# Nearest-neighbour upsampling on one core: the first load as two DMAs over alternate partitions

## The chip, the cores and the metric

The kernel runs on one core of one Trainium2 chip. The metric is the device time of one execution in microseconds (us). Three runs of the kernel before gave 196.85, 196.99 and 197.22 us; their median, 196.99 us, is the time that the change is measured against.

Of the core's engines the kernel uses VectorE (DVE in the profile) and ScalarE (ACT) for copies inside the on-chip memory, and SyncE (SP) to issue DMAs, the transfers between the device memory and the on-chip memory. A DMA is carried out by 16 DMA engines that work beside the compute engines.

## The reference

The input `x` has the shape 16 x 64 x 64 x 64 in float32 (16.78 MB). Each element is repeated twice along the height and twice along the width, so that the output is 16 x 64 x 128 x 128 (67.11 MB):

```python
for i in range(new_h):
    for j in range(new_w):
        result[:, :, i, j] = x[:, :, i // scale_factor, j // scale_factor]
```

Nothing is computed with the numbers. Each is read once and written four times.

## The kernel before, in words

**Layout.** All 65,536 image rows (16 x 64 x 64, of 64 elements each) are dealt out to the 128 partitions of the on-chip memory: partition p holds R = 512 rows in succession, 128 KB of the input, and the output that belongs to them is 512 KB in succession. One tile, `mem`, takes the whole work: the input lies at its end (`xt`), and the space ahead of it (79 rows' worth of output, `FREE`) and the space of input rows that are used up hold expanded rows.

**Loads.** Four DMAs on SP's queue (lines 192 to 197) bring the input in, cut by rows: rows 0 to 31 (`HEAD`, 8 KB per partition, 1.05 MB in all), rows 32 to 255 and 256 to 479 (56 KB per partition, 7.34 MB each), and rows 480 to 511 (1.05 MB). Each of them covers all 128 partitions. They wait for nothing.

**Nine steps.** The rows are worked on in nine blocks (`rows`, line 181: 52, 40, 52, 63, 52, 64, 63, 63 and 63). For a block, VectorE expands the first 9/16 of its rows (line 215) and ScalarE the rest (line 216) into a region `u` of `mem`, and one DMA on SP's queue stores the region (line 217). The regions of even blocks lie at the start of `mem`, those of odd blocks just ahead of the input rows that are still to be used, so that a block's copies wait for the store that last read their region and for the rows that they read. The first store is also made to wait for the third load, `loads[-2]` (lines 218 to 226), so that stores begin when nearly all of the input is in.

**Order.** The tile framework puts a wait on each instruction for what it reads or overwrites. One step written by hand bears on the change: `begin_before_barrier` (line 11) takes the first `EARLY` instructions of SP, asserts that each is a DMA without a wait, and moves them ahead of the barrier at which the program's engines meet at its start. With `EARLY = 4` those are the four loads. `close_early` (line 74) shapes the end: the closing barrier and most of the clearing of semaphores happen while the last stores are still under way, and the last instruction, on SP, waits for the last store to land.

A DMA has its own semaphore, and what depends on it waits for that. The semaphores for DMAs are eight, used in turn: DMA number n takes number n modulo 8.

Of the kernel before, what the change touches and what calls it, by code (L numbers as in the profile page):

```python
# [6 lines left out]

EARLY = 4  # L10


def begin_before_barrier(nc):
# [5 lines left out]
    sp = mybir.EngineType.SP  # L19
    loads = [i for i in body.instructions if i.engine == sp][:EARLY]  # L20
    for load in loads:
# [132 lines left out]
@with_exitstack  # L154
def kernel(
    ctx: ExitStack,
    tc: tile.TileContext,
    x: bass.AP,
    scale_factor: int,
    out: bass.AP,  # L160
):
    nc = tc.nc
    nc.at_finalize(begin_before_barrier)
    nc.at_finalize(close_early)
    P = nc.NUM_PARTITIONS
    s = int(scale_factor)
    B, C, H, W = x.shape
    R = B * C * H // P
    fdt = x.dtype

    xp = x.rearrange("b c h w -> (b c h) w").rearrange("(p r) w -> p r w", p=P)
    op = out.rearrange("b c (h hd) w -> (b c h) (hd w)", hd=s).rearrange(
        "(p r) w -> p r w", p=P
    )

    rows = [52, 40, 52, 63, 52, 64, 63, 63, 63]
    GROW = s * s
    FREE = 79
    WF = FREE * GROW * W
    assert sum(rows) == R
    mem_pool = ctx.enter_context(tc.tile_pool(name="mem", bufs=1))
    mem = mem_pool.tile([P, WF + R * W], fdt, name="mem")
    xt = mem[:, WF:].rearrange("p (r w) -> p r w", r=R)

    HEAD = 32
    cuts = [0, HEAD, R // 2, R - 32, R]
    loads = [
        nc.sync.dma_start(out=xt[:, lo:hi], in_=xp[:, lo:hi])  # L195
        for lo, hi in zip(cuts, cuts[1:])
    ]

    def expanded(r0, r1):
        return (  # L200
            xt[:, r0:r1].unsqueeze(2).unsqueeze(4).to_broadcast([P, r1 - r0, s, W, s])
        )

    r0 = 0
    before = (0, 0)
    for n, k in enumerate(rows):
        size = k * GROW * W
        at = 0 if n % 2 == 0 else WF + r0 * W - size
        assert at >= before[1] or at + size <= before[0]
        before = (at, at + size)  # L210
        u = mem[:, at : at + size].rearrange(
            "p (k a w b) -> p k a w b", k=k, a=s, w=W
        )
        kv = k * 9 // 16
        nc.vector.tensor_copy(out=u[:, :kv], in_=expanded(r0, r0 + kv))  # L215
        nc.scalar.copy(out=u[:, kv:], in_=expanded(r0 + kv, r0 + k))  # L216
        store = nc.sync.dma_start(out=op[:, r0 : r0 + k, :], in_=u)  # L217
        if n == 0:
            tc.add_manual_dep(
                store.ins,  # L220
                loads[-2].ins.name,
                mybir.DependencyInfo(
                    mybir.DependencyClass.Sync, mybir.DependencyReason.DATA
                ),
                reason="stores begin as the loads end",
            )
        r0 += k
# [35 lines left out]
```

## Time and profile before

| | |
|---|---|
| median of three runs | 196.99 us (196.85 to 197.22) |
| the profiled execution | 197.0 us |
| its span, first to last instruction | 195.7 us |
| bytes moved by DMA | 83.89 MB, 429 GB/s over the span |
| share of 16 DMA engines' span taken by packets | 99.3% |
| VectorE busy | 69.7 us (36%), 9 copies |
| ScalarE busy | 51.4 us (26%), 9 copies and a table load |
| issue of the four loads on SP | 0.00 to 2.02 us; 383 to 632 ns each, median 434 |
| first VectorE copy begins | 4.59 us |
| first store issued | 38.52 us |

The profiled execution agrees with the median of the runs, and 1.3 us of it lie outside its span. The span runs from SP's first DMA issue to the end of the last wait on SP. Where the profile gives the DMA share over a short stretch, a packet counts wholly in the slice in which it begins; a value over 1 followed by a zero is such a packet. Each packet of data is one partition's piece of one DMA; the packets under 512 B are the signals that tell a semaphore of a DMA's end, 16 for each DMA.

### The profile page before, as it was taken

What the parts mean: (1) busy time and instruction counts of PE and PEld (TensorE: products, weight loads), DVE (VectorE), ACT (ScalarE), POOL (GpSimd) and SP (SyncE); (2) the same over time, 40 slices, a digit from 0 to 9 for tenths busy, and PEclk for the clock granted to TensorE, in tenths of its full rate; (3) what the DMA queues carried; (4) which work ended last, traced back from release to release, by engine and by line L of the source; (5) the groups of instructions that cost most, each with busy time, mean ns of one, the idle gap of its engine ahead of it and who ended that gap; (6) DMA issues with size and microseconds to landing.
All of it is one profiled execution on the core that took longest, in us unless ns stands there. A gap on an engine that the chain in (4) does not pass through costs nothing.

```text
span 195.7 us, 105 instructions
## 1 busy us (share of the span) xinstructions
DVE 69.7 (36%) x9; ACT 51.4 (26%) x10; POOL 0.2 (0%) x4
## 2 busy tenths in 40 slices
DVE  0950600000039299069008205930692079100000
ACT  0000595000036093064910006666000074000000
POOL 0000000000000000000000000000000000000000
DMA  9899889799899989899999899999999999999994
GB/s 402 375 481 457 375 375 563 310 440 523 348 442 452 526 348 512 359 422 422 422 422 523 348 523 429 429 429 429 422 422 422 422 422 422 528 514 422 435 422 211
DMA packets 1872, 83.89 MB, mean 429 GB/s; under 512 B 208, under 2 KB 208, under 8 KB 208
## 3 DMA queue, kind: packets, MB, share of 16 engines
q1 hardware_dynamic: 1872, 83.89, 99.3%
HBM read 16.78 MB, written 67.11 MB: 429 GB/s over the span
## 4 chain that ended last, share of the span: by engine, by line
DMA 67%; DVE 18%; SPq 0%; issue 0%; DVEq 0%
DMA out_dram<-mem 48%; DMA mem<-in_x_dram 19%; DVE mem L215 18%; SPq L195 0%; DVEq L215 0%; SPq L217 0%
## 5 line engine op out<-in xcount | busy, mean ns | idle before, releaser
L215 DVE COPY mem<-mem 128x8960 f32<-128x8960 f32 (+3 forms) x9 | 69.7, 7740 | 97.5 <-DMA out_dram<-mem 83.9
L216 ACT COPY mem<-mem 128x7168 f32<-128x7168 f32 (+2 forms) x9 | 50.1, 5572 | 90.8 <-DMA out_dram<-mem 84.3
L216 ACT ACT_TABLE_LOAD x1 | 1.3, 1283 | 21.6 <-DMA mem<-in_x_dram 21.6
L244 POOL MEMSET const-bfloat16-1.0<- 128x1 bf16 x1 | 0.1, 102 | 0.0
L244 POOL MEMSET const-uint8-127<- 128x1 uint8 x1 | 0.1, 102 | 0.0
L244 POOL MEMSET const-float32-0.0<- 128x1 f32 x1 | 0.1, 99 | 0.2 <-issue 0.2
L244 POOL MEMSET const-float32-1.0<- 128x1 f32 x1 | 0.1, 99 | 0.0
## 6 DMA issues: line engine op xcount, KB each, us to landing
out_dram<-mem SPq DMA_DIRECT2D x4, 8064.0 KB, 28.4
out_dram<-mem SPq DMA_DIRECT2D x3, 6656.0 KB, 19.7
mem<-in_x_dram SPq DMA_DIRECT2D x2, 7168.0 KB, 29.3
out_dram<-mem SPq DMA_DIRECT2D x1, 5120.0 KB, 29.8
mem<-in_x_dram SPq DMA_DIRECT2D x2, 1024.0 KB, 22.1
out_dram<-mem SPq DMA_DIRECT2D x1, 29.9
```

What stands on the lines that cost most here:

```text
L215: nc.vector.tensor_copy(out=u[:, :kv], in_=expanded(r0, r0 + kv))
L216: nc.scalar.copy(out=u[:, kv:], in_=expanded(r0 + kv, r0 + k))
L244: nc = _bacc.Bacc("TRN2", target_bir_lowering=False, num_devices=1)
```

## The change

The load of rows 0 to 31 becomes two DMAs. The first covers the even partitions (0, 2, ... 126), the second the odd ones (1, 3, ... 127), 64 pieces of 8 KB each. The other three loads stay as they are, as do the copies and the stores. `loads` now holds only those three, and `loads[-2]` is still the load of rows 256 to 479. `EARLY` goes from 4 to 5, so that all five loads go ahead of the opening barrier.

```diff
-EARLY = 4
+EARLY = 5
...
     HEAD = 32
     cuts = [0, HEAD, R // 2, R - 32, R]
+    for odd in range(2):
+        nc.sync.dma_start(out=xt[odd::2, :HEAD], in_=xp[odd::2, :HEAD])
     loads = [
         nc.sync.dma_start(out=xt[:, lo:hi], in_=xp[:, lo:hi])
-        for lo, hi in zip(cuts, cuts[1:])
+        for lo, hi in zip(cuts[1:], cuts[2:])
     ]
```

The order of instructions on VectorE, ScalarE and GpSimd is unchanged. The first copy on VectorE now waits for two DMAs in place of one, the first use of ScalarE likewise waits for one more, the first store names two more semaphores among its waits and the second store one fewer. SP issues 14 DMAs in place of 13.

## Prediction

> **What bounds the kernel now.** I read the page's engine rows, its DMA queue row, the chain that ended last, then the waits, and last short stretches of time at the start, where the change lies.
>
> ```profile
> span 195.7 us, 105 instructions
> DVE 69.7 (36%) x9; ACT 51.4 (26%) x10; POOL 0.2 (0%) x4
> DMA  9899889799899989899999899999999999999994
> ...
> q1 hardware_dynamic: 1872, 83.89, 99.3%
> HBM read 16.78 MB, written 67.11 MB: 429 GB/s over the span
> ...
> DMA 67%; DVE 18%; SPq 0%; issue 0%; DVEq 0%
> ```
>
> No compute engine is busy for 40% of the span, but packets fill 99.3% of the 16 DMA engines' time. The chain gives VectorE 18%, but that is time in which the queues still hold another store: the DMA row has no slice under 7 before the last. So the kernel ends when the DMA engines have moved 83.89 MB, and an edit is worth what it changes of three things: when they start, how fast they run, and how long the last landing takes.
>
> ```profile
> core 0: us, DVE busy (x) ACT busy (x) POOL busy (x), PEclk, DMA share, GB/s
> 0.00:1.00 1.00, 0.00 (x0) 0.00 (x0) 0.20 (x4) 1.00 0.00 0
> 1.00:2.00 1.00, 0.00 (x0) 0.00 (x0) 0.00 (x0) 1.00 1.01 229
> 2.00:3.00 1.00, 0.00 (x0) 0.00 (x0) 0.00 (x0) 1.00 1.01 426
> 3.00:4.00 1.00, 0.00 (x0) 0.00 (x0) 0.00 (x0) 1.00 1.06 451
> 4.00:8.00 4.00, 3.41 (x1) 0.00 (x0) 0.00 (x0) 1.00 1.03 444
> ...
> 140.00:194.00 54.00, 17.67 (x2) 6.16 (x1) 0.00 (x0) 1.00 1.01 440
> ```
>
> These stretches show the start: nothing moves for 1 us after the first issue, then a microsecond at 229 GB/s in which the engines are all busy but their packets slow, and from 2 us on the steady rate. Loads (2 to 38 us) and stores (after 41) run at the same rate, and pieces of 8 KB at the same as pieces of 64 KB. What limits an engine is thus common to reading and writing device memory and is no cost per packet: it is the engine itself (429 / 16 = 26.8 GB/s each) or its way into the on-chip memory.
>
> ```profile
> L195 SPq DMA_DIRECT2D mem<-in_x_dram x4: 383/434/632, 0.0 to 1.4; - x4
> ...
> DVE mem L215 <- DMA mem<-in_x_dram: 13.6, 2, 9.0
> ACT L216 <- DMA mem<-in_x_dram: 21.6, 1, 21.6
> ...
> SPq L217 <- DMA mem<-in_x_dram: 36.1, 1, 36.1
> ```
>
> The first row is the issue of the loads on SP (shortest, median, longest in ns). The others are waits (total us, times, longest): VectorE, after its first copy, idles 9.0 us for the second load; SP waits 36.1 us until the third load lands and the first store may go.
>
> **The change part by part.**
>
> *One more issue on SP, ahead of the barrier.* One issue by the median row is 0.43 us. The other loads are issued that much later, and the barrier opens at about 2.5 us in place of 2.1. The second part of the head is issued at about 0.4 us, and by the row of the first load (issue at 0, data from 1.0 us) its data can move from about 1.4 us; half the head takes 0.52 MB / 429 GB/s = 1.2 us and is not through before 2.2. So the gap between them is covered by some 0.8 us. The next load, needed at about 4 us, is issued by 0.9. The barrier covers nothing that is needed before 4.59 us, where VectorE's first copy starts. If the cover were gone, each of these would cost up to its 0.43 us. Price: 0.
>
> *One more semaphore and its waits.* VectorE's first copy and ScalarE's first instruction get one more wait. The chain shows what waits cost to pass: 0.08 us lie between the third load's landing at 38.44 us and the first store's issue at 38.52. VectorE has 9.0 us of idle time behind the copy. The first store's added waits are for DMAs that ended 34 us earlier; if they delay it by 0.1 us, the fourth load, 1.05 MB or 2.4 us of queued work, covers it. The second store loses a wait, and its issue too lies behind a queued store. The 16 extra end-of-DMA packets: the 208 that exist lie inside 99.3% of busy time at an overall 429 GB/s, so the whole difference to the 440 of the late stretch, spread over 13 DMAs, would be 195.7 x (1 - 429/440) / 13 = 0.38 us per DMA. That bound holds the start and the tail too, so the true price is far lower. Price: 0, with 0.38 as upper end.
>
> *An earlier start of the streams.* The first DMA has 64 pieces to prepare in place of 128. If preparing them sets the start, half of the first issue of 383 ns, 0.19 us, comes off. If the start is a fixed delay, nothing does. A gain above 0.38 us would need the whole issue to vanish. I take 0.1 us, bounds 0 and -0.38.
>
> *How the head's 1.05 MB spread over the ways into memory.* This is the term that decides. Every DMA in the trace covers all 128 partitions in sequence, so no row shows a transfer that leaves out every other partition. Lower bound: the spread over 16 engines and their ways into memory stays even, each half takes 0.52 MB / 429 GB/s, together 2.44 us as now: 0. [...] I take +2.1, between these two, and the side of sharing rather than of the even spread. The nearest row, the load of all partitions, speaks for the even spread, but the equal rate of loads and stores leaves a limit at the way into memory possible, and the partition pattern is the one thing that changes for it. This is a judgement, and the lower bound stays in the range.
>
> [...]
>
> *Sum.* 0 + 0 - 0.1 + 2.1 = +2.0 us. The transfers are back to back from here to the end, the queues never run empty, and no engine idles for want of the delayed data except where it idles already; the delay goes whole into the end. Profiled execution: 195.7 + 2.0 = 197.7 of span, + 1.3 outside it = 199.0 us. That execution's 197.0 is the median of the runs, so 199.0 stands for those too.
>
> **The rivals.**
>
> *Even spread, hidden edit (the other side).* The halves move at full rate and only the start counts: 196.99 - 0.1, between 196.6 and 197.35 us. For it: 99.3% of busy time and covers everywhere. Against it: nothing that a row shows, only the untested pattern. It decides if the stretch from 2 to 4 us stays above 400 GB/s.
>
> *An earlier start that counts.* If preparation sets both the 1.0 us of silence and the spread of the first packets, half the first issue for each, 0.19 + 0.19 us, gives 196.6 us or a little less. Against it: the silence is 1.0 us where the issue is 0.38, so most of it is a delay after the issue.
>
> *A gap between the halves.* The second half's data come later than the 1.4 us reckoned above; past 2.2 us the engines stand idle. One issue late (0.43 us), or a whole silence of 1.0 us less the cover: 197.4 to 198.0 us. Against it: the cover of 0.8 us, and loads already follow each other without a gap.
>
> **How the numbers follow.** Shared ways 52%, even spread 28%, a gap or other small loss 10%, earlier start 10%. The likeliest gives 199.0 us, its own range 198.3 to 199.5. 0.2% is 0.39 us, about what a measurement of this kernel can tell from no change. The range reaches to the even spread: 196.6 to 199.5, leaving out most of the earlier start and the outer ends. Faster: the earlier start and an edge of the even spread, 0.11; same: 0.28; slower: the shared ways and the gap, 0.61.
>
> **What the profile after would show.** If I am right, the stretch from 2 to 4 us falls to 200 to 300 GB/s, VectorE's first copy starts at about 6.5 us in place of 4.59, the third load lands at about 40.5 in place of 38.44, and the stores keep their rate. If 2 to 4 us stay at 430 and the first copy starts by 4.6, the spread is even and the forecast is wrong by its largest term. A zero in the DMA share near 2.5 us would be the gap.

## The result, and the profile after

The changed kernel takes 199.16 us (median of six runs, 198.66 to 199.39) where the kernel before took 197.05 (196.85 to 197.22, six runs). The ratio is 1.0105, 95% interval 1.0092 to 1.0118: 2.1 us slower. The profiled execution of the changed kernel is the fastest of its six, 198.66 us with a span of 197.3. The traces therefore explain 1.65 us of the 2.1; the rest of the median isn't in a trace.

The page of the changed kernel, in the same rows as shown of the kernel before:

```profile
span 197.3 us, 107 instructions
DVE 69.7 (35%) x9; ACT 51.4 (26%) x10; POOL 0.2 (0%) x4
DMA  9988988998999998999999799999999999999994
...
q1 hardware_dynamic: 1888, 83.89, 98.8%
HBM read 16.78 MB, written 67.11 MB: 425 GB/s over the span
```

The compute engines do the same work in the same time. The kernel is still bound by its DMA engines, which are 98.8% busy in place of 99.3% in a longer span. The 16 more packets are the signals of the fourteenth DMA.

The stretches at the start of the changed kernel (length, busy time of three engines, clock, share of the DMA engines, GB/s):

```profile
core 0: us, DVE busy (x) ACT busy (x) POOL busy (x), PEclk, DMA share, GB/s
0.00:1.00 1.00, 0.00 (x0) 0.00 (x0) 0.20 (x4) 1.00 0.00 0
1.00:2.00 1.00, 0.00 (x0) 0.00 (x0) 0.00 (x0) 1.00 0.71 139
2.00:3.00 1.00, 0.00 (x0) 0.00 (x0) 0.00 (x0) 1.00 0.94 377
3.00:4.00 1.00, 0.00 (x0) 0.00 (x0) 0.00 (x0) 1.00 1.09 451
```

The forecast wanted 200 to 300 GB/s between 2 and 4 us. The trace has 377 and 451, against 426 and 451 before. The halves of the head move at full rate. What differs is the microsecond before, 139 in place of 229 GB/s: the data start later, the first packet at 1.33 us in place of 1.02. Two rows on SP's issues show a part of the reason, first the two halves, then the three loads behind them (shortest, median, longest in ns; first and last start):

```profile
L195 SPq DMA_DIRECT2D mem<-in_x_dram x2: 551/564/578, 0.0 to 0.6; - x2
```

```profile
L197 SPq DMA_DIRECT2D mem<-in_x_dram x3: 432/446/586, 1.2 to 2.3; - x3
```

The issue of half the partitions takes longer than that of all of them, 551 ns where the first load took 383. That is 0.17 us of the 0.30 us by which the first packet is later; the rest passes between the end of the issue and the data. And the first large load (rows 32 to 255) is issued at 1.2 us in place of 0.43.

Next the moment when the DMA engines pass from the head to that large load, in stretches of 0.4 us. A large share marks the start of large packets. Before:

```profile
3.80:4.20 0.40, 0.00 (x0) 0.00 (x0) 0.00 (x0) 1.00 5.32 2294
4.20:4.60 0.40, 0.01 (x1) 0.00 (x0) 0.00 (x0) 1.00 0.33 143
```

After:

```profile
3.80:4.20 0.40, 0.00 (x0) 0.00 (x0) 0.00 (x0) 1.00 0.83 348
4.20:4.60 0.40, 0.00 (x0) 0.00 (x0) 0.00 (x0) 1.00 3.15 1086
4.60:5.00 0.40, 0.00 (x0) 0.00 (x0) 0.00 (x0) 1.00 3.01 1004
5.00:5.40 0.40, 0.24 (x1) 0.00 (x0) 0.00 (x0) 1.00 0.76 287
```

Before, nearly all of the engines begin the large load within 0.4 us. After, they straggle over more than 0.8 us. The packet records of the trace say what the stragglers do. A record doesn't name its DMA engine, but on one engine each packet begins 3 ns before the one ahead of it ends, so the records can be strung together. Across a gap this doesn't work: which of the waiting engines takes the next packet is a choice, and the longest gap depends on it, but the sum of the gaps doesn't. Start + duration in ns; `s` is a DMA's end signal; a gap stands in brackets:

```
before, one engine     3844+309  4150+9s          4156+2116  6269+2116  8382+2116
after, one engine      3931+309  4237+9s  [821]   5067+2324  7387+2173  [43] 9603+2168
after, another         4015+309  4321+9s          4327+2465  6788+2427  9211+2116
```

Before, there is no gap, and each 57 KB packet takes 2116 ns from the first one on. After, some engines stand idle for up to 0.7 or 0.8 us between head and large load, and the first one or two large packets of an engine take up to 3129 ns. Past the first ones of each engine, most head packets take the usual 309 ns and few over 330, and there is no gap between the halves. Over the 16 engines, idle time in the first 10 us comes to 0.24 us on average and excess packet time, over each size's steady duration and without the first packet, to 0.76 us (before: none, and 0.05). Engines begin 0.31 us later at the median (1.15 and 1.46 us). 0.31 + 0.24 + 0.71 = 1.26 us, of which the slow packets are the largest part. Another 0.13 us are lost later, and the engines end 1.46 us later at the median, the slowest 1.65 us later.

The chain that ended last carries this on. Its step for the load of rows 256 to 479, for which the first store waits, from start and duration (us), before and after:

```profile
0.91 37.52 DMA mem<-in_x_dram
```

```profile
1.85 37.96 DMA mem<-in_x_dram
```

It lands 1.38 us later (39.81 and 38.43 us), and the stores follow from there.

### The profile page after: what moved, and what is told of

The parts are those of the page before. It is cut to its first block, busy times and chain, and to the rows that moved or that the text cites. A ratio compares the mean times of both kernels' runs of the same rounds, so it can differ in the third digit from the quotient of the medians.

```text
span 197.3 us, 107 instructions
## 1 busy us (share of the span) xinstructions
DVE 69.7 (35%) x9; ACT 51.4 (26%) x10; POOL 0.2 (0%) x4
## 2 busy tenths in 40 slices
DMA packets 1888, 83.89 MB, mean 425 GB/s; under 512 B 224, under 2 KB 224, under 8 KB 224
## 3 DMA queue, kind: packets, MB, share of 16 engines
q1 hardware_dynamic: 1888, 83.89, 98.8%
## 4 chain that ended last, share of the span: by engine, by line
DMA 67%; DVE 18%; SPq 1%; issue 0%; DVEq 0%
DMA out_dram<-mem 47%; DMA mem<-in_x_dram 19%; DVE mem L217 18%; SPq L195 1%; SPq L197 0%; DVEq L217 0%; SPq L219 0%
```

## The experiments

Each run's ratio is against runs of the kernel before on the same chip. Diffs are against the changed kernel unless said otherwise.

**Rows in place of partitions.** Is it the number of DMAs or the pattern of 64 partitions?

```diff
-    for odd in range(2):
-        nc.sync.dma_start(out=xt[odd::2, :HEAD], in_=xp[odd::2, :HEAD])
+    for lo, hi in ((0, HEAD // 2), (HEAD // 2, HEAD)):
+        nc.sync.dma_start(out=xt[:, lo:hi], in_=xp[:, lo:hi])
```

> Two head DMAs cut by rows (16 rows each, all 128 partitions) in place of even and odd partitions; as many DMAs and packets per engine order as in the changed kernel but for pieces of 4 KB. Theory P (the pattern of 64 alternate partitions is what costs): the issues fall back to about 0.43 us, the first packets begin at about 1.0 us, the time is 196.8 to 197.4 us. Theory N (any further DMA in front of the large loads makes their pieces late at the DMA engines): 198.5 to 199.3 us, with idle DMA time near 4 to 5 us. Theory S (shared ways into memory, the forecast): 196.8 to 197.4 us, since all partitions are covered.

Measured: 197.59 us, ratio 1.0028 (1.0014 to 1.0042), just above the range of theories P and S, and far below that of N. The issues take 373 and 424 ns, the first packet begins at 1.0 us, and the large load is issued at 0.89. One engine's first large packet takes 2860 ns; most of the others are at or near 2116. Idle time in the first 10 us is 0.07 us on average and excess packet time 0.36, against 0.24 and 0.76 in the changed kernel, though this version has twice as many head packets, of 4 KB. The large load is third in line here too, but is issued 0.34 us earlier.

**Halves in sequence.** Is it the step of two?

```diff
-    for odd in range(2):
-        nc.sync.dma_start(out=xt[odd::2, :HEAD], in_=xp[odd::2, :HEAD])
+    for half in range(2):
+        at = slice(half * 64, half * 64 + 64)
+        nc.sync.dma_start(out=xt[at, :HEAD], in_=xp[at, :HEAD])
```

> Head DMAs over partitions 0 to 63 and 64 to 127, in sequence, in place of even and odd. Theory P, if the step of two is what costs: issues of about 0.4 us and 196.8 to 197.5 us; if 64 partitions in place of 128 are what costs: issues of about 0.55 us and 198.5 to 199.3 us, as in the changed kernel. Theory N: 198.5 to 199.3 us whatever the issues take. Theory S: a half reaches fewer ways into memory than all partitions do, packets of 8 KB take about 0.6 us in place of 0.31, and the time is 199.0 to 199.7 us.

Measured: 199.25 us, ratio 1.0108 (1.0092 to 1.0123). The same time as the changed kernel, but for the most part not for the same reason:

```profile
2.00:3.00 1.00, 0.00 (x0) 0.00 (x0) 0.00 (x0) 1.00 1.09 303
3.00:4.00 1.00, 0.00 (x0) 0.00 (x0) 0.00 (x0) 1.00 0.97 221
4.00:5.00 1.00, 0.00 (x0) 0.00 (x0) 0.00 (x0) 1.00 1.09 246
```

The engines are busy throughout, but the rate falls, and from 3 us on it is about half the usual one (221 GB/s between 3 and 4 us, against 451 before). The 8 KB packets of the second half take 495 to 648 ns in place of 309. This is what the forecast expected of alternate partitions, and here it is real: without each engine's first one, the head's packets take 1.6 us per engine more than at 309 ns. The late start (1.34 us) and slow first large packets (up to 2882 ns) come on top. The issues take 557 and 577 ns, so that the longer issue belongs to 64 partitions and not to the step. What slows the second half's packets, these runs don't show.

**The second load split.** The head is whole again; alternate partitions are used where 7.34 MB move by them.

```diff
+    nc.sync.dma_start(out=xt[:, :HEAD], in_=xp[:, :HEAD])
     for odd in range(2):
-        nc.sync.dma_start(out=xt[odd::2, :HEAD], in_=xp[odd::2, :HEAD])
+        nc.sync.dma_start(
+            out=xt[odd::2, HEAD : R // 2], in_=xp[odd::2, HEAD : R // 2]
+        )
...
-        for lo, hi in zip(cuts[1:], cuts[2:])
+        for lo, hi in zip(cuts[2:], cuts[3:])
```

> The head is one DMA again; the load of rows 32 to 255 is cut into even and odd partitions. Theory P: the two slow issues lie under the head's 2.4 us of data, so 196.9 to 197.5 us. Theory N: the pieces behind the head come late as in the changed kernel, 198 to 199.3 us. Theory S: 7.34 MB at half the rate, some 17 us longer, 214 us.

Measured: 197.01 us, ratio 1.0001 (0.9991 to 1.0010). No cost at all. From 8 to 12 us, in the middle of the split load, the rate is that of the kernel before; the kernel before first, then this run:

```profile
8.00:12.00 4.00, 4.00 (x1) 0.00 (x0) 0.00 (x0) 1.00 1.06 459
```

```profile
8.00:12.00 4.00, 0.00 (x0) 0.00 (x0) 0.00 (x0) 1.00 1.06 459
```

Every 57 KB packet of the split load takes 2116 to 2121 ns. Theory S, the forecast's, falls: alternate partitions load here at the rate of all of them. VectorE's first copy waited until 21.7 us in this kernel and the time didn't move, which shows how much slack the compute engines have.

**A head of 64 rows.** More data in front of the large load:

```diff
-    HEAD = 32
+    HEAD = 64
```

> The changed kernel with a head of 64 rows in place of 32, so that each half takes twice as long to move and the issue of the large load behind it has 2.4 us more of cover. Theory P and theory N, if lateness of the large load's pieces is the cost: the idle time near 4 to 5 us goes, the later first packet (0.3 us) stays: 197.2 to 197.7 us. If the price is fixed per stepped DMA, or sits in the pace of the packets that follow: 198.8 to 199.3 us as in the changed kernel. Theory S: twice the bytes at half the rate, 201 to 202 us.

Measured: 197.82 us, ratio 1.0035 (1.0021 to 1.0048), a little over the range of P and N and far from the others. The engines pass to the large load without a gap, and each of its 49 KB packets takes 1815 ns from the first on. Of the 1.05% of the changed kernel, two thirds are gone.

**Heads of 40 and of 24 rows.** The same edit with 40 and 24, for the size of the effect.

> Even and odd partitions as in the changed kernel, head of 40 rows in place of 32: 0.61 us more of data in front of the first large load. Theory L (late: pieces of the large load reach the DMA engines only 3.0 to 3.8 us after its issue begins at 1.2 us, that is between 4.2 and 5.1 us): the head now ends between 4.8 and 5.4 us, the idle gaps are all but gone, 197.7 to 198.3 us. Theory F (a fixed price of two 64-partition DMAs at the start): 198.9 to 199.4 us.

Measured: 198.01 us, ratio 1.0043 (1.0028 to 1.0058). Theory L holds, F falls: 0.61 us more of cover (data in front of the large load) bring back 1.2 us.

> Even and odd partitions, head of 24 rows: 0.61 us less of data in front of the first large load. Theory L: 0.6 us more of idle time than the changed kernel, 199.5 to 200.0 us. Theory F: 198.9 to 199.4 us. VectorE's first copy now also needs the large load and starts at about 23 us, which its idle time covers under both theories.

Measured: 199.36 us, ratio 1.0115 (1.0100 to 1.0130), short of the range of L and inside that of F, which the run with 40 rows had ruled out. In the trace, of the slowest of the four runs, the head is through by 4.2 us, eight engines pass without a gap, the others wait; that is 0.69 us of idle time on average over the 16, and the longest wait is over 2 us. The first large packets take up to 3712 ns where 2192 is the steady time. So the loss per 0.61 us of head isn't linear: it is large between 40 and 32 rows and small below.

**One whole head, small and large.** The kernel before with 16 and with 64 rows:

```diff
 # against the kernel before
-    HEAD = 32
+    HEAD = 16
```

> The kernel before with a head of 16 rows in one DMA over all partitions: no 64-partition DMA anywhere, but 1.2 us less of data in front of the large load, which is issued at 0.43 us. Theory L, if lateness is a matter of time since issue alone: pieces come between 3.4 and 4.3 us, the head is through at about 2.8 to 3.0, so 0.5 to 1.3 us idle, 197.5 to 198.3 us. Theory F, and theory L if only 64-partition DMAs in front make the next load late: 196.9 to 197.3 us.

Measured: 197.17 us, ratio 1.0001 (0.9991 to 1.0011). The large load is issued at 0.43 us and needed between 2.6 and 3.0, and it is in time: of its first packets all but five take the steady 2267 ns, the longest 2452. That is 2.2 to 2.6 us after its issue began, where the changed kernel's large load is late 3.0 us and more after its own. Lateness is thus no matter of time since issue alone.

> The kernel before with a head of 64 rows in one DMA: the counterpart of the run with even and odd partitions and 64 rows, which took 0.6 us more than the kernel before. All theories: 196.9 to 197.3 us, so that the 0.6 us belong to the two 64-partition DMAs and not to the head's size. If 197.5 us or more, the head's size is part of it.

Measured: 197.45 us, ratio 1.0011 (1.0001 to 1.0022). This lies between the two cases of the forecast. A whole head of 64 rows costs next to nothing, so that of the 0.35% with two halves some 0.24% belong to the halves.

**Rows again, with less cover.** The version by rows with a head of 24, so that no DMA covers 64 partitions but the large load is third in line:

```diff
 # against the version by rows
-    HEAD = 32
+    HEAD = 24
```

> Head of 24 rows as two DMAs over all 128 partitions, 12 rows each: the large load is the third DMA in line, as in the changed kernel, and has less data in front of it, but no 64-partition DMA. Theory K (64-partition DMAs in front hold up the load behind them): no gap, 197.2 to 197.8 us, as with rows and a head of 32. Theory C (the third DMA in line is late when little data lies in front): idle time at 3.4 to 5 us as with alternate partitions and 24 rows, 198.5 to 199.8 us.

Measured: 198.81 us, ratio 1.0083 (1.0067 to 1.0098). Theory C holds, and K as it was put falls: the third DMA is late without any 64-partition DMA in front. Two engines wait for its first packet, 2.15 us together, and the others' second packets take up to 2459 ns where 2192 is steady. The 64-partition DMAs do add to it, or their later third issue does (1.24 us against 0.89): with this same head of 24 rows, idle time and excess packet time in the first 10 us are 0.17 and 0.37 us on average here, and 0.69 and 1.01 with alternate partitions. The wait of a few engines reaches all of them: the first store waits for the load of rows 256 to 479 to land whole, is issued at 40.13 us in place of 38.52, and between 38 and 45 us the engines stand idle for 0.41 us on average (0.01 before, and 0.01 in the changed kernel, which doesn't have this second loss).

**One half ahead.** The large load second in line, behind the even half; the odd half follows it:

```diff
-    for odd in range(2):
-        nc.sync.dma_start(out=xt[odd::2, :HEAD], in_=xp[odd::2, :HEAD])
+    nc.sync.dma_start(out=xt[0::2, :HEAD], in_=xp[0::2, :HEAD])
+    nc.sync.dma_start(out=xt[:, HEAD : R // 2], in_=xp[:, HEAD : R // 2])
+    nc.sync.dma_start(out=xt[1::2, :HEAD], in_=xp[1::2, :HEAD])
...
-        for lo, hi in zip(cuts[1:], cuts[2:])
+        for lo, hi in zip(cuts[2:], cuts[3:])
```

> Only the even half of the head stands in front of the large load; the odd half is issued behind it. Theory K with a price per DMA: the large load, issued at 0.6 us and needed at 3.0 to 3.4, is late by some 0.3 to 0.6 us, and the first packet is 0.3 us later than before: 197.8 to 198.5 us. If it takes two 64-partition DMAs to hold up a load: only the later start, 197.3 to 197.7 us. If the price is fixed once a 64-partition DMA leads: 198.9 to 199.4 us.

Measured: 197.63 us, ratio 1.0019 (1.0009 to 1.0028).

```profile
1.00:2.00 1.00, 0.00 (x0) 0.00 (x0) 0.00 (x0) 1.00 0.51 131
2.00:3.00 1.00, 0.00 (x0) 0.00 (x0) 0.00 (x0) 1.00 1.36 549
3.00:4.00 1.00, 0.00 (x0) 0.00 (x0) 0.00 (x0) 1.00 1.79 762
4.00:5.00 1.00, 0.00 (x0) 0.00 (x0) 0.00 (x0) 1.00 0.00 0
5.00:6.00 1.00, 0.00 (x0) 0.00 (x0) 0.00 (x0) 1.00 2.12 918
```

The large packets begin together at about 3 us and again at about 5: nobody straggles. Only 1.2 us of data lie in front of the large load, half as much as in the changed kernel, and it still comes in time, second in line and issued at about 0.6 us. Of the three cases, the time fits the one with only the later start. What is left, 0.4 us, goes with that start: the first packet comes at 1.33 us in place of 1.02, and the median engine begins at 1.65 us in place of 1.15.

**Four ahead.** The head's halves cut once more by rows, so that the large load is fifth:

```diff
-EARLY = 5
+EARLY = 7
...
-    for odd in range(2):
-        nc.sync.dma_start(out=xt[odd::2, :HEAD], in_=xp[odd::2, :HEAD])
+    for lo, hi in ((0, HEAD // 2), (HEAD // 2, HEAD)):
+        for odd in range(2):
+            nc.sync.dma_start(out=xt[odd::2, lo:hi], in_=xp[odd::2, lo:hi])
```

> The head of 32 rows as four 64-partition DMAs (even and odd partitions of rows 0 to 15, then of rows 16 to 31): the same data in front of the large load, twice the DMAs. Theory K with a price per DMA: the large load is held up by twice as much, its pieces come at 6 to 8 us where they are needed at 4.2 to 4.8: 200.5 to 203 us. A fixed price: 198.9 to 199.5 us.

Measured: 200.35 us (199.49 to 200.87), ratio 1.0170 (1.0147 to 1.0192), just below the range of theory K and above that of a fixed price. The profiled execution is the fastest of the four, 199.49 us.

```profile
2.00:3.00 1.00, 0.00 (x0) 0.00 (x0) 0.00 (x0) 1.00 1.01 406
3.00:4.00 1.00, 0.00 (x0) 0.00 (x0) 0.00 (x0) 1.00 0.80 180
4.00:5.00 1.00, 0.00 (x0) 0.00 (x0) 0.00 (x0) 1.00 0.90 332
```

The rate is full while the first two DMAs last, and falls to 180 GB/s at 3 us, when the third is due. Here the third DMA is a small one over 64 partitions, and it is late too: most engines wait some 0.3 us or more for it.

**A small third DMA.** The changed kernel with rows 32 to 63 as a DMA of their own over all partitions:

```diff
-EARLY = 5
+EARLY = 6
...
-    cuts = [0, HEAD, R // 2, R - 32, R]
+    cuts = [0, HEAD, 2 * HEAD, R // 2, R - 32, R]
```

> The changed kernel with the next 32 rows as a DMA of their own over all partitions: the third DMA has pieces of 8 KB in place of 56, and the large load, now fourth, has 2.4 us more data in front. Theory K, whatever the size of the held-up load: its 8 KB pieces come late too, 198.6 to 199.4 us. If only large pieces come late: the third follows without a gap and the fourth has time enough, 197.6 to 198.1 us.

Measured: 198.92 us, ratio 1.0091 (1.0074 to 1.0107). This is in the range of theory K. The third DMA has 8 KB packets and is late all the same: some engines wait for its first packet, for up to about 0.7 us, and single packets of it take up to 1378 ns. So it isn't only large packets that come late.

No version tried is faster than the kernel before.

## Why the total was right and its reason wrong

199.0 us was forecast and 199.16 measured, inside the range, and the direction was right. The working behind it was not: a term of 2.1 us that doesn't exist stood in for a loss that had been priced at nothing, and that the two are of one size is luck.

*How the head's 1.05 MB spread* (+2.1 us) is the step that failed. The forecast counted on shared ways into memory, and so on 200 to 300 GB/s between 2 and 4 us. No run shows the 2.1 us for alternate partitions; they were the author's estimate. In their place the runs showed no loss: the split second load costs nothing (ratio 1.0001, packets of 2116 to 2121 ns), and past each engine's first one most of the head's packets take 309 ns as before. The true value is the lower bound, zero. The row nearest to it, the load over all partitions, had said so; the forecast passed it over because equal rates for loads and stores left a limit at the way into memory possible. A rate cut to about half exists, as the halves in sequence show (221 and 246 GB/s between 3 and 5 us), but for a pattern that the change doesn't have. The forecast's own test said the same at once: 2 to 4 us stayed above 400 GB/s (377 and 451, 414 over both), and VectorE's first copy began at 5.16 us, nearer to 4.59 than to the 6.5 forecast.

*One more issue on SP* was priced at zero, and behind it is where most of the time went. The step took 0.43 us for an issue, and had the next load issued by 0.9 us and so covered. An issue over 64 partitions takes 0.55 to 0.58 us, the large load goes out at 1.23 us, and it is third in line; its packets begin as late as 5.07 us, though it is needed from 4.2, and its first ones are slow (0.24 and 0.71 us on average). The first load's 1.0 us from issue to data was used as if it held for every load. For the third it doesn't.

*An earlier start* (-0.1 us) had the wrong sign: +0.31 us at the median engine, with the longer issue. In the version with one half ahead, where little else is lost, a start 0.50 us later at the median engine goes with 0.4 us of the total.

*More waits* at zero were right as far as the runs show. After its first copy VectorE stands idle for 9.8 us in the changed kernel, and before the first store SP waits 34.7 us for the load of rows 256 to 479, long after the head's DMAs have ended.

*The delay goes whole into the end*: right. The load of rows 256 to 479 lands 1.38 us later, and the span is 1.6 us longer.

Of the rivals, *a gap between the halves* was nearest in kind, idle engines that wait for late data. It sat one DMA too early, between the halves, where no gap is, and its 0.4 to 1.0 us was too small. It had 10%.

What is shown: the kernels with a whole head lose 0.11% at most; with alternate partitions the loss shrinks from 2.1 to 0.7 us as the head grows from 32 to 64 rows; with the cut by rows it is 0.28% at 32 rows and 0.83% at 24; and all but 0.4 us of it goes when the large load moves up to second place. What stays open is what makes the third late. In every kernel with late packets the late DMA is third or later in line, but it was also issued at 0.89 us or after, and its issue was still under way when the first data moved (1.0 to 1.3 us). The second DMA was in time in all of them, issued at 0.42 to 0.62 us. Place in line and issue before the data start aren't separated by these runs, nor is the part of 64 partitions as such from that of the later issue that comes with them. And they don't show why the first large packets are slow also on engines without a gap, which is the largest part of the loss in the trace; these slow packets come and go with the lateness, though (0.04 us of excess with a head of 64 rows, 0.10 with one half ahead).

## What to carry to other kernels

When DMA engines are the bound (99.3% busy here before the change), a split at the head of the queue isn't free because its bytes are few (1.05 of 83.89 MB here, and it cost 2.1 us): ask when the DMA behind it is issued, how much data covers it, and whether it was second in line before. In these runs two small DMAs in front of a large one needed more data in them than one did: over alternate partitions 2.45 us of data were too little and 4.9 us were enough for the large one to come in time, where 1.2 us in one whole DMA sufficed. And a forecast that hits the total has to be checked at its own markers, since two unlike causes gave the same 2.1 us here: late and slow packets of the large load in the changed kernel, and slow head packets with the halves in sequence.

## What the runs showed that was not expected

- Issuing a DMA over 64 partitions takes longer than over 128: 492 to 597 ns against 372 to 435 for the first two DMAs of the kernels that begin with two of all 128. The issue over 128 partitions right behind one over 64 is long too, 567 to 648 ns.
- Alternate partitions load at the full rate (2116 ns for 57 KB packets in the split second load), halves in sequence at about half of it (495 to 648 ns for 8 KB in the second half, in place of 309).
- A few late engines can delay all of them a second time, at the first store, which waits for the whole load of rows 256 to 479: 0.41 us on average with rows and a head of 24, 0.01 in the changed kernel.
